# Seven modulation units of the second block's first layer move from TensorE to VectorE

## The chip, the cores and the metric

The kernel runs on one core of a Trainium2 chip. Its engines are TensorE (PE: matmuls, and PEld: the loading of the stationary operand), VectorE (DVE), ScalarE (ACT), GpSimd (POOL), and SyncE (SP), which here issues the loads from device memory. The metric is the device time of one execution in microseconds (us), the median of several runs; less is better.

## The reference, cut to what matters

Two transformer blocks of two layers each run one after the other on 256 latent tokens of width 1024, in float32. The second block also carries 256 context tokens through its first layer and is modulated: each of its layers computes six vectors of 1024 values for the latent tokens and six for the context from a condition vector, and these shift and scale the norms and gate the residual sums.

```python
for l in range(2):                       # second block
    mod_l = split(silu(c)     @ ada_w[l] + ada_b[l], 6)   # 1024 x 6144 weights
    mod_c = split(silu(c_ctx) @ ada_w[l] + ada_b[l], 6)
    hl = modulate(x_lat, norm_g[l, 0], mod_l[0], mod_l[1])
    hc = modulate(x_ctx, norm_g[l, 0], mod_c[0], mod_c[1])
    mix_c, mix_l = mixer(hc, hl, ...)    # l = 0: mLSTM + window attention; l = 1: global + neighbourhood
    x_lat = x_lat + mod_l[2] * (mix_l @ w_out[l])
    x_lat = x_lat + mod_l[5] * conv_ffn(modulate(x_lat, norm_g[l, 1], mod_l[3], mod_l[4]), ...)
    # x_ctx likewise with mod_c, in layer 0 alone
```

The condition vectors do not depend on the tokens, so the modulation can be computed at any time before its use, also while the first block runs.

## The kernel before, in words

**Stages.** The program is one long list of steps: attention 0 (to 160.7 us of the profiled span, where the next stage's first `gr` stands), the first block's FFN 0 (to 333), attention 1 (to 478), FFN 1 (to 694), the second block's first mixer (mLSTM heads 0 to 3 with their transposed outputs at 786.3, 825.1, 860.9 and 890.8, window attention and output projections, to 961), its FFN (to 1309), the second mixer (to 1520) and the last FFN.

**Weights.** All matmul weights come in units of at most 128 x 1056 floats, in the order of their first use (`fetch`, from L481). Each unit is loaded by SP into a `raw` buffer, split by ACT into a rounded high part `wh` (L496) and by DVE into the low part `wl` (L497), each with four buffers, and PE multiplies three products, high by high, high by low and low by high (L501). So each weight unit costs an instruction of about a microsecond on ACT and on DVE, and PE runs behind them by some units.

**Modulation.** Layer 0's 6144 columns are 24 units of 256 columns (the second layer has 24 more). A unit is computed in one of two ways. On PE (`p_ada`, from L599; the units named in `ADA_PE`, 13 to 19): two weight units are fetched and split, 16 matmuls 256 wide multiply them with the condition (`csil`), ACT copies the row (`adarow`, L616), two small matmuls turn it into columns, and DVE adds the bias (L621). On DVE (`ada_upto`, from L567): the unit is two blocks of 128 columns, whose transposed weights (`adaw`, 128 x 1024) SP loads unsplit, and for each block DVE runs two reductions over 1024 elements (L591), one for the latent and one for the context condition. These have three `adaw` buffers, two in FFN 1.

**Where the units stand.** The table `ADA` says how many units each slot takes, in order: slots `a0.0` to `a0.3` are woven into the four groups of attention 0, `f0` into FFN 0, `f1` into FFN 1, `e.0` to `e.2` into mLSTM heads 0 to 2 of the second block, and `f2` into its FFN. `ada_need` (L564) adds what a later step cannot do without: FFN 0's side list begins with `ada_need(0, 8)`, then the context's norm and modulation (`ctx_norm`), then slot `f0`.

**The order.** The program is built with `schedule_with_timeline_sim=True`: at build time a scheduler reorders the instructions of each engine by its own estimate of their times, with the list of steps as priority. A change of one step so moves others around it. On the chip each engine works through its list strictly in order.

**The mLSTM heads.** `core` (L1479) and `decay` (L1431) of a head are a chain: NM transposes on PE, W on DVE and ACT, W times the scores on DVE, the products `o` on PE, `hs` on DVE, a power on POOL, `hs` again, and the transposes `ht` (L1527). Beside head h stand steps that do not depend on it (`fill`): projections of the next heads, output projections, PE's modulation units, and beside head 3 the projections of the window attention's q.

Of the kernel before, what the change touches and what calls it, by code (L numbers as in the profile page):

```python
# [36 lines left out]

UNITS_AHEAD = 4
RAW_BUFS = 4
ADA_PE = range(13, 20)  # L40
HI_BUFS = 4
LO_BUFS = 4
CUTS = 1
# [4 lines left out]
def _ar(a, n):  # L48
    return np.arange(a, a + n)
# [6 lines left out]
def unit_specs():  # L56
# [7 lines left out]
    def halves(key, w, l, cols):  # L64
        for kh in range(2):
            add(key + (kh,), w, l, _ar(512 * kh, 512), cols)
# [12 lines left out]

    for i in ADA_PE:  # L80
        halves(("ada", 0, i), "ada_w_2", 0, _ar(256 * i, 256))
# [225 lines left out]
def weave(a, b, tail=0):  # L307
# [7 lines left out]


ADA = {
    "a0.0": 0, "a0.1": 1, "a0.2": 1, "a0.3": 2, "f0": 1, "f1": 4, "e.0": 3, "e.1": 2, "e.2": 2, "f2": 28,
}


# [55 lines left out]
class Prog:  # L377
# [189 lines left out]
    def ada_upto(self, n, room=True):  # L567
# [3 lines left out]
        for i in range(a, self.ada_at):  # L571
            if i in ADA_PE:
                out += self.p_ada(i // 24, i % 24)
# [1332 lines left out]
```

## Time and profile before

| | us |
|---|---|
| median of three runs | 1708.85 (1705.65 to 1709.5) |
| the profiled execution's own time | 1709.56 |
| its span, first to last instruction | 1707.8 |
| PE, PEld, DVE, ACT, POOL busy in the span | 1653.7, 1561.7, 1373.0, 953.9, 59.0 |

The span is what the trace covers; 1.8 us lie outside it. A matmul's record is longer than the distance to the next matmul's start, since matmuls are pipelined; what a matmul costs a busy PE is that distance. The same holds to a lesser degree of DVE.

### The profile page before, as it was taken

Reading aid. Unit: us, or ns where it says so; the run is one execution under the profiler, and the core shown is the slowest. Engines: PE = TensorE matmul, PEld = TensorE weight load, DVE = VectorE, ACT = ScalarE, POOL = GpSimd, SP = SyncE. Lnnn points to the kernel's source line nnn. Section 1 sums busy time; section 2 is a strip of 40 time slices with the busy share of each in tenths; the row PEclk is TensorE's granted clock in tenths of the full one; section 3 lists DMA queues with packets and bytes.
Section 4 is the critical chain, followed back from the end, with each engine's and each line's share of the span. In section 5 each row is a group of like instructions: output and inputs, shape, how many; then the busy total and the mean of one; then the engine's idle time right before and its main releaser. Section 6 shows DMA issues by size and latency. Waiting matters only on the chain.

```text
span 1707.8 us, 31978 instructions
## 1 busy us (share of the span) xinstructions
PE 1653.7 (97%) x12336; PEld 1561.7 (91%) x12336; DVE 1373.0 (80%) x2832; ACT 953.9 (56%) x1693; POOL 59.0 (3%) x75
## 2 busy tenths in 40 slices
PE   7999999999899999999989999999999999999999
PEld 7999999999899999899978997888889999899999
DVE  6798999887787887767687788998887864679887
ACT  6666555656677667555446653233335554666554
POOL 0000000000100000100010000000000210000000
PEclk9999999999999999999989999999999999999999
DMA  8446675554455564524421454757745521235663
GB/s 308 134 140 232 219 239 190 180 173 138 137 173 162 186 197 147 165 73 157 140 75 42 154 176 151 231 180 235 264 151 158 197 82 57 75 112 173 191 193 124
DMA packets 80664, 277.97 MB, mean 163 GB/s; under 512 B 8960, under 2 KB 12160, under 8 KB 80256
## 3 DMA queue, kind: packets, MB, share of 16 engines
q1 hardware_dynamic: 79216, 273.30, 49.6%
q10 hardware_dynamic: 1296, 2.62, 0.4%
q8 instruction: 97, 1.59, 0.4%
q14 instruction: 55, 0.45, 0.1%
HBM read 274.84 MB, written 1.05 MB: 162 GB/s over the span
## 4 chain that ended last, share of the span: by engine, by line
PE 62%; DVE 6%; ACT 3%; issue 1%; POOL 0%; DVEq 0%; ACTq 0%; POOLq 0%
PE acc L501 41%; PE s L501 15%; PE o L501 4%; DVE wl L497 2%; PE ptp L821 1%; ACT wh L496 1%; ACT L1028 1%; DVE nt L1145 0%; DVE cc L1026 0%; PE stv L501 0%; POOL rs L661 0%; PE tt L741 0%; ACT L1380 0%; PE tt L837 0%; DVE g L640 0%
## 5 line engine op out<-in xcount | busy, mean ns | idle before, releaser
L496 ACT ACTIVATE wh<-raw 128x1024 fp32r<-128x1024 f32 (+4 forms) x446 | 454.0, 1025 | 443.9 <-PE acc L501 291.3
L497 DVE TENSOR_TENSOR wl<-raw,wh 128x1024 fp32r<-128x1024 f32 (+4 forms) x446 | 524.6, 1181 | 114.1 <-ACT wh L496 111.2
L501 PE MATMUL acc<-nh,wh 128*128 128x256 f32 (+2 forms) x872 | 268.0, 308 | 4.2 <-DVE ug L1618 1.9
L501 PE MATMUL acc<-nh,wl 128*128 128x256 f32 (+2 forms) x872 | 268.1, 308 | 0.8 <-DVE wl L497 0.7
L501 PE MATMUL acc<-nl,wh 128*128 128x256 f32 (+2 forms) x872 | 266.6, 306 | 0.0
L501 PE MATMUL acc<-wh,nh 128*128 128x256 f32 (+2 forms) x768 | 220.5, 288 | 12.1 <-ACT nh L642 7.9
L501 PE MATMUL s<-nh,wh 128*128 128x256 f32 (+2 forms) x744 | 224.2, 301 | 0.9 <-ACT wh L496 0.9
L501 PE MATMUL s<-nh,wl 128*128 128x256 f32 (+2 forms) x744 | 223.4, 300 | 0.0
L501 PE MATMUL s<-nl,wh 128*128 128x256 f32 (+2 forms) x744 | 223.1, 300 | 0.0
L501 PE MATMUL acc<-wh,nl 128*128 128x256 f32 (+2 forms) x768 | 219.5, 288 | 2.2 <-DVE nl L1148 2.1
L501 PE MATMUL acc<-wl,nh 128*128 128x256 f32 (+2 forms) x768 | 218.7, 286 | 0.3 <-DVE wl L497 0.3
L501 PE MATMUL acc<-g,wh 128*128 128x256 f32 x1056 | 187.1, 281 | 5.2 <-ACT g L639 2.7
L501 PEld LDWEIGHTS acc<-nh,wh 128*128 128x128 f32 x872 | 164.2, 188 | 13.6 <-ACT nh L1147 2.1
L501 PEld LDWEIGHTS acc<-nh,wl 128*128 128x128 f32 x872 | 164.1, 188 | 10.0 <-DVE wl L497 1.4
L501 PEld LDWEIGHTS acc<-nl,wh 128*128 128x128 f32 x872 | 164.2, 189 | 8.3
L591 DVE CUSTOM_DVE_ANT_0 junk<-adaw,sil,c0t 128x1024 f32<-128x1024 f32 x132 | 168.8, 1278 | 0.2
L501 PEld LDWEIGHTS acc<-g,wh 128*128 128x128 f32 x1056 | 160.3, 189 | 7.7 <-ACT g L639 3.6
L501 PEld LDWEIGHTS acc<-wh,nh 128*128 128x128 f32 x768 | 147.6, 192 | 14.0 <-ACT nh L642 8.2
L501 PEld LDWEIGHTS acc<-wh,nl 128*128 128x128 f32 x768 | 147.7, 193 | 4.5 <-DVE nl L1148 3.0
L501 PEld LDWEIGHTS acc<-wl,nh 128*128 128x128 f32 x768 | 147.4, 192 | 1.3 <-DVE wl L497 0.7
L501 PEld LDWEIGHTS s<-nh,wh 128*128 128x128 f32 x744 | 139.8, 188 | 7.4 <-ACT wh L496 1.1
L501 PEld LDWEIGHTS s<-nl,wh 128*128 128x128 f32 x744 | 139.9, 188 | 6.1
(385 smaller groups left out, 3338.9 us busy)
## 6 DMA issues: line engine op xcount, KB each, us to landing
raw<-in_wts SPq DMA_DIRECT2D x342, 512.0 KB, 4.1
adaw<-in_ada SPq DMA_DIRECT2D x82, 512.0 KB, 4.4
raw<-in_wts SPq DMA_DIRECT2D x72, 448.0 KB, 3.4
raw<-in_wts SPq DMA_DIRECT2D x24, 384.0 KB, 3.1
x<-in_x SPq DMA_DIRECT2D x8, 256.0 KB, 6.6
raw<-in_wts SPq DMA_DIRECT2D x4, 408.0 KB, 3.5
rpb<-in_rpb ACTq DMA_DIRECT2D x1, 1536.0 KB, 8.8
raw<-in_wts SPq DMA_DIRECT2D x2, 528.0 KB, 3.9
```

The costliest lines, as they stand in the source:

```text
L496: nc.scalar.activation(hf[:, c], raw[:, c], AF.Copy)
L497: self.last_wl = nc.vector.tensor_sub(lf[:, c], raw[:, c], hf[:, c].bitcast(F32)).ins
L501: self.nc.tensor.matmul(o, a, b, start=start, stop=stop)
L591: self.nc.vector.tensor_tensor_reduce(out=junk, in0=tiles[j], in1=self.sil[:, c], scale=1.0, scalar=self.C["adab%d" % l][:, m:m + 1], op0= ...
L821: self.nc.tensor.transpose(pt[:, kb], P[:, kb * 128:(kb + 1) * 128], self.ident)
L1028: nc.scalar.activation(cc, cc, AF.Silu)
```

## The change

`ADA_PE` becomes empty, so no unit of the modulation is computed on PE, and `ADA` gives the seven units to DVE in earlier slots:

```diff
-ADA_PE = range(13, 20)
+ADA_PE = ()
 ADA = {
-    "a0.0": 0, "a0.1": 1, "a0.2": 1, "a0.3": 2, "f0": 1, "f1": 4, "e.0": 3, "e.1": 2, "e.2": 2, "f2": 28,
+    "a0.0": 2, "a0.1": 2, "a0.2": 2, "a0.3": 2, "f0": 4, "f1": 8, "f2": 28,
 }
```

| units computed in | attention 0 | FFN 0 | FFN 1 | mixer 1 (PE before) | FFN of the second block |
|---|---|---|---|---|---|
| before | 4 | 5 (4 by `ada_need`) | 4 | 7 | 28 |
| now | 8 | 4 | 8 | 0 | 28 |

Since eight units are done by the end of attention 0, `ada_need(0, 8)` adds nothing, and `ctx_norm` is the first step of FFN 0's side list. From the second block's FFN on, units and steps are the same.

In the built program DVE has 160 reductions of L591 where it had 132, and 14 fewer `wl`; ACT has 14 fewer `wh` and 7 fewer `adarow`; PE has 112 matmuls with `csil` and 14 small ones with `adarow` fewer. Reductions on DVE between the same neighbours of the program (the `on` of L833 and the `gr` of L1023, at these times in the trace of before):

| stretch | 55.1 to 82 | to 111 | to 138.2 | to 160.7 | to 190.5 | to 277.4 | 488.3 to 523.2 | to 560.3 | to 668.4 |
|---|---|---|---|---|---|---|---|---|---|
| before | 0 | 7 | 9 | 0 | 5 | 11 | 2 | 4 | 10 |
| now | 9 | 9 | 12 | 2 | 2 | 10 | 6 | 6 | 20 |

The first place is DVE at the end of attention 0, around the last pair of heads' `on` (L833), whose transposes become the last part of the mix (`mixl3`) and release the last output projection, whose sums are the L843 rows. Before:

```order
L831 RECIPROCAL rec_1792<-rsum_1524 128x4
L843 TENSOR_TENSOR x3_80<-x3_80,acc_1859 128x256
L497 TENSOR_TENSOR wl_1856<-raw_1853,wh_1855 128x1024
L833 TENSOR_TENSOR on_1794<-o_1523,rec_1792 128x256
L640 TENSOR_TENSOR mixl3_175<-tt_1796,mixh3_171 128x256
L843 TENSOR_TENSOR x0_77<-x0_77,acc_1885 128x256
L843 TENSOR_TENSOR x0_77<-x0_77,acc_1897 128x256
```

And now:

```order
L843 TENSOR_TENSOR x3_80<-x3_80,acc_1899 128x256
L497 TENSOR_TENSOR wl_1896<-raw_1893,wh_1895 128x1024
L831 RECIPROCAL rec_1832<-rsum_1564 128x4
L591 ISA junk_1606,mods0_148<-adaw_1596,sil_131,c0t_87 128x1024
L591 ISA mods0_148 128x1
L833 TENSOR_TENSOR on_1834<-o_1563,rec_1832 128x256
L591 ISA junk_1645,mods0_148<-adaw_1601,sil_131,c0t_87 128x1024
```

One reduction stands directly ahead of that `on`, and two more follow it, one of them ahead of `mixl3` and one behind it.

The second place is PE in mLSTM head 3, from its second group of NM transposes on (`wh_11210` with `nh` is the projection of the window attention's q, `exh` and `exl` with `wh_11193` the output projection of heads 0 and 1, `o` the products of head 3). Before:

```order
L1441 MATMUL NM_11335<-c0t_87,an_5856 128x128 x4
L501 MATMUL acc_11556<-wh_11210,nl1_141 128x256
L501 MATMUL acc_11556<-wh_11210,nh2_134 128x256
L501 MATMUL acc_11556<-wl_11211,nh2_134 128x256
L501 MATMUL acc_11556<-wh_11210,nl2_142 128x256
L501 MATMUL o_11415<-vx_11021,W_11318 128x129 x2
L501 MATMUL acc_11556<-wh_11210,nh3_135 128x256
```

And now:

```order
L1441 MATMUL NM_11167<-c0t_87,an_5886 128x128 x4
L501 MATMUL acc_11506<-exl_11096,wh_11193 128x512
L501 MATMUL acc_11506<-exh_11095,wl_11194 128x512
L501 MATMUL acc_11540<-exl_11096,wh_11193 128x512
L501 MATMUL acc_11540<-exh_11095,wl_11194 128x512
L501 MATMUL o_11247<-vx_10927,W_11150 128x129 x2
L501 MATMUL acc_11575<-exh_11095,wh_11193 128x512
L501 MATMUL acc_11575<-exl_11096,wh_11193 128x512
L501 MATMUL acc_11575<-exh_11095,wl_11194 128x512
L501 MATMUL o_11247<-vx_10927,W_11150 128x129
```

All 77 matmuls of the q projections that stood between the transposes `ht` of head 2 and of head 3 now stand ahead of head 2's, in the places that the `csil` matmuls have left.

## Rows read from the trace of the kernel before

**Rows 1.** The page's part 1: busy us, share of the span, instructions.

```profile
PE 1653.7 (97%) x12336; PEld 1561.7 (91%) x12336; DVE 1373.0 (80%) x2832; ACT 953.9 (56%) x1693; POOL 59.0 (3%) x75
```

**Rows 2.** Busy time by stretch, attention 0 and FFN 0; columns in its first line.

```profile
core 0: us, PE busy (x) PEld busy (x) DVE busy (x) ACT busy (x) POOL busy (x), PEclk, DMA share, GB/s
55.10:82.00 26.90, 26.90 (x233) 26.90 (x232) 16.90 (x40) 18.94 (x44) 0.00 (x0) 1.00 0.42 137
82.00:111.00 29.00, 29.00 (x253) 29.00 (x252) 25.37 (x57) 19.25 (x44) 0.00 (x0) 1.00 0.47 146
111.00:138.20 27.20, 25.88 (x217) 24.77 (x215) 26.68 (x66) 16.03 (x37) 0.00 (x0) 1.00 0.56 178
138.20:160.70 22.50, 20.54 (x171) 19.85 (x171) 17.98 (x39) 15.72 (x31) 1.96 (x2) 1.00 0.66 232
160.70:190.50 29.80, 29.30 (x258) 29.30 (x259) 29.80 (x56) 18.63 (x29) 0.00 (x0) 1.00 0.73 232
190.50:277.40 86.90, 85.52 (x740) 84.61 (x740) 81.50 (x146) 47.00 (x69) 0.87 (x1) 1.00 0.67 216
```

**Rows 3.** Busy time by stretch, FFN 1.

```profile
488.30:523.20 34.90, 33.45 (x279) 32.41 (x278) 32.31 (x76) 28.32 (x46) 0.00 (x0) 1.00 0.53 180
523.20:560.30 37.10, 34.41 (x277) 33.76 (x277) 27.86 (x55) 23.38 (x38) 0.00 (x0) 0.95 0.53 167
560.30:668.40 108.10, 105.53 (x897) 104.03 (x896) 89.01 (x177) 80.45 (x122) 0.00 (x0) 1.00 0.55 176
```

**Rows 4.** Busy time by stretch, mLSTM heads 1 to 3 and what follows.

```profile
786.30:825.10 38.80, 38.80 (x274) 36.02 (x273) 24.52 (x60) 18.98 (x42) 1.11 (x2) 1.00 0.37 121
825.10:860.90 35.80, 35.46 (x254) 33.03 (x253) 29.66 (x77) 16.92 (x38) 1.01 (x1) 1.00 0.35 118
860.90:890.80 29.90, 23.72 (x162) 21.08 (x160) 24.58 (x81) 14.51 (x38) 3.08 (x3) 0.93 0.27 89
890.80:943.90 53.10, 51.10 (x342) 45.34 (x342) 39.12 (x122) 28.78 (x64) 1.17 (x1) 0.94 0.12 41
```

**Rows 5.** PE's timeline in mLSTM: start us, length us, operation, count.

```profile
766.80 0.28 PE L501 MATMUL acc<-wl,csil 128*128 128x256 f32 x1
766.92 0.28 PE L501 MATMUL acc<-wh,csil 128*128 128x256 f32 x1
...
772.64 0.50 PE L501 MATMUL acc<-c0t,adarow 128*128 128x2 f32 x4
773.00 0.36 PE L501 MATMUL acc<-wl,csil 128*128 128x256 f32 x1
```

**Rows 6.** A group of PE from 764 to 848: busy us, mean ns; idle before.

```profile
L501 PE MATMUL acc<-wl,csil 128*128 128x256 f32 x56 | 14.0, 285 | 0.0
```

**Rows 7.** Groups of ACT and of DVE from 764 to 848.

```profile
L496 ACT ACTIVATE wh<-raw 128x1024 fp32r<-128x1024 f32 x24 | 25.1, 1056 | 28.8 <-PE acc L501 25.0 <-DVE mods L621 1.3 <-DVE wl L497 1.3
...
L497 DVE TENSOR_TENSOR wl<-raw,wh 128x1024 fp32r<-128x1024 f32 x24 | 29.1, 1223 | 6.8 <-ACT wh L496 6.0 <-PE acc L501 0.6
```

**Rows 8.** DVE's timeline in attention 0: a reduction and its read.

```profile
115.28 1.28 DVE L591 CUSTOM_DVE_ANT_0 junk<-adaw,sil,c0t 128x1024 f32<-128x1024 f32 x1
116.48 0.08 DVE L591 DVE_READ_ACCUMULATOR2_ANT mods<- 128x1 f32 x1
```

**Rows 9.** Waits from 55 to 191: us in total, times, longest.

```profile
DVE wl L497 <- ACT wh L496: 11.3, 11, 2.9
```

**Rows 10.** Groups from 860.9 to 890.8, head 3.

```profile
L501 PE MATMUL acc<-wh,nh 128*128 128x256 f32 x26 | 7.4, 285 | 0.0
...
L497 DVE TENSOR_TENSOR wl<-raw,wh 128x1024 fp32r<-128x1024 f32 x5 | 6.1, 1220 | 0.7 <-ACT wh L496 0.6
```

**Rows 11.** Busy time in slices of 10 us, around head 3's end.

```profile
880.00:890.00 10.00, 7.14 (x33) 5.55 (x31) 7.42 (x36) 3.07 (x13) 0.64 (x1) 0.84 0.00 0
890.00:900.00 10.00, 8.42 (x31) 6.50 (x32) 9.15 (x25) 4.23 (x10) 1.97 (x2) 0.66 0.00 0
```

**Rows 12.** Groups of DVE from 256 to 268, the context's modulation.

```profile
L1145 DVE SCALAR_TENSOR_TENSOR nt<-x,gs,bc 128x256 f32<-128x256 f32 x8 | 3.5, 474 | 0.0
```

## The prediction, made before the changed kernel ran

> **What bounds the kernel now.** I read the page's busy times first, then the busy times of stretches, then timelines. The page says PE 97% busy and its weight loads 91%, DVE 80%, ACT 56% [rows 1]: on average TensorE is the bound, and work that leaves it should pay. The average hides stretches with another bound, and this change takes work out of one and puts it into others.
>
> In the mLSTM heads, which the seven units leave, PE has no gap through head 1 (38.80 of 38.8) and almost none through head 2 (35.46 of 35.8), while DVE is busy for 24.52 and 29.66 [rows 4]. There PE decides. Head 3 is otherwise: PE 23.72 of 29.9, DVE 24.58 of 29.9 [rows 4]: neither is full, a chain between them decides.
>
> In attention 0, which gains eight blocks, PE is full until 111 and DVE is not: 16.90 of 26.9, then 25.37 of 29.0. From 111 to 138.2 it is turned round: DVE 26.68 of 27.2, and PE misses 1.3. In FFN 0 DVE has no free moment up to 190.5 (29.80 of 29.8), after that 81.50 of 86.9, with PE at 85.52 [rows 2]. FFN 1, which also gains eight blocks, has more room on DVE: idle 2.6 of 34.9, 9.2 of 37.1 and 19.1 of 108.1 us, PE nearly full [rows 3].
>
> **What the change removes.** A `csil` matmul's record is 285 ns long, 56 of one kind and 56 of the other [rows 6], which would make 32 us. But they start 0.12 us apart [rows 5], and that is what a full PE gets back: 112 x 0.12 = 13.4. The row's four small matmuls take 0.36 from start to start [rows 5], seven times 2.5. Together 15.9 us of PE. Beside it go 14 splits on ACT (1056 ns) and on DVE (1223 ns) [rows 7], 14.8 and 17.1 us, off the path in heads 1 and 2, where both engines have gaps. Weights of as many bytes are now loaded as `adaw`; DMA is at 0.27 to 0.73 of its time in all stretches concerned [rows 2 to 4], and the loads run ahead by several buffers, so I price them at nothing; where this cover fails, SP's list stands still at an `adaw` whose buffer DVE has not read, and the weights behind it come late, which would add to the DVE terms below.
>
> **What the heads give back.** PE is full only as long as there is something to fill it with. The scheduler has put other projections where the `csil` matmuls stood, and takes them from later. Counted in the program's order with the distance above (narrow is a matmul 256 columns wide, wide one of 512):
> - Up to head 0's transposes: 48 `csil` go, 43 narrow and 9 wide projection matmuls come: nothing.
> - Head 1: 32 `csil` and their small ones go, 38 narrow and 3 wide come, 9 wide go: 1.3 less. PE is without a gap before and should be after: -1.3.
> - Head 2: 32 `csil`, the small ones, 4 narrow and 3 wide go, 5.9 less: PE 29.6 where it had 35.46. But DVE keeps its conversions and needs 29.66 [rows 4]. With both at about 30, waits between them show; I take 32 for 35.8: -4. Bounds: -5.9 by PE alone; nothing, if the 6 us that DVE waits now stay beside 29.66.
> - Head 3: the 77 matmuls of the q projections go (9.3 us; a third of them is the row of 26 in [rows 10]), and with them 5 conversions of DVE, 6.1 us [rows 10]. PE then has 14.4, DVE 18.5. DVE waits now for 29.9 - 24.58 = 5.3; if that stays, the head takes 23.8: -6. [...] I charge 1 us: -5. Bounds: -8 (DVE's 18.5 and 3.4 us of waits) and +5.1 (the clock falls to half for the whole head and its 14.4 us all lie on the chain: 14.4 more, less the 9.3 that PE no longer has to do).
>
> Sum -10.3, bounds -15.9 (all of PE's work) and +3.8 (head 1's -1.3, nothing in head 2, +5.1 in head 3). What follows head 3 stands in the same order as before, and I change nothing there.
>
> [...]
>
> **What attention 0 pays.** One reduction occupies DVE for 1.20 us (115.28 to 116.48), though its record is 1.28 long; with the read behind it I count 1.21 [rows 8]. By the counts in the table of the change:
> - 55.1 to 82: 9 more, 10.9 us, where DVE is idle for 10.0 [rows 2]: 0.9 over. That idle time is mostly conversions that wait for ACT, 11.3 us between 55 and 191 [rows 9], and these waits shrink as DVE falls behind.
> - 82 to 111: 2 more, 2.4, into 3.6 idle.
> - 111 to 138.2: 3 more, 3.6, into 0.5.
>
> Together 16.9 into 14.1: DVE needs 85.9 us where 83.1 are. If it never waited, the last pair's `on` would come 2.8 later. If every present wait stayed, 16.9 later. DVE does best at 98% (111 to 138.2) and 94% (190.5 to 277.4) [rows 2]; at 96% the 85.9 become 89.5: 6.4 late. PE cannot cover this: behind `on` come the last part of the mix, the output projection, the sums and the norm, all before FFN 0's first matmul, so what is late there is late for good. Two more reductions follow `on`, 2.4 us, in a stretch with 4.5 us idle [rows 2] and half hidden by the transposes: 0.5. FFN 0's start has the context's modulation now, 16 instructions of some 0.4 us start to start (474 ns records, [rows 12]), 6.4, against 3 reductions fewer, 3.6: 2.8 more on a full DVE; PE runs behind conversions by some units and takes this up, about 1 us of it shows. Later FFN 0 loses that modulation, and with it most of the 1.4 us that PE misses from 190.5 to 277.4 [rows 2]: -1. I take +6.5 for all this; bounds 2.8 (no wait is left) and 16.9 (every wait stays).
>
> **What FFN 1 pays.** 16 more, 19.4 us, into 30.9 idle. Only the first stretch is over: 4 more, 4.9, into 2.6 [rows 3], 2.3 over; the stretch after has 9.2 idle and gets 2.4. The third goes from 89.01 to 101.1 of 108.1, 94%, a load at which FFN 0's PE misses 1.6% [rows 2]. PE there misses 2.6 now. +2, bounds 0 and 6 (all of the overflow, and 3.5 more of PE's waits in the third stretch).
>
> **Sum.** -10.3 + 6.5 + 2 = -1.8 on the profiled execution's 1709.56: 1707.8. The median of the runs lies 0.7 below that execution, so the median of the changed kernel should be 1707. Two large terms of opposite sign nearly cancel; that is the forecast.
>
> **Rivals.**
> 1. *All of PE's work comes back.* TensorE is 97% busy, DVE 80% [rows 1]. [...] By rows: heads -14, attention 0 only its overflow 2.8, FFN 1 nothing: 1698 on the median's scale. For it: the scheduler knows the new lists and fills DVE's gaps. Against it: head 3 was not PE's before, and 111 to 138.2 is DVE's.
> 2. *DVE becomes the bound of attention 0*, the other side. The place is the last pair's `on`; it decides from the point where DVE's waits between 55.1 and 138.2 stay above 7 us beside the 16.9 added. Then `on` is 10 late, FFN 0's start 2 more, and with FFN 1 at 4 and the heads at -8 the kernel takes 8 longer: 1717. For it: DVE is at 98% before the three reductions come, the softmax of four heads runs through it, and each pair of reductions is 2.4 us in which nothing else gets done. Against it: PE has no gap up to 111 while DVE waits [rows 2], so that a DVE that falls a little behind starves nobody there at first.
> 3. *The heads' chain eats the gain.* Head 3, bared of its fill, stays at 29.9 because of the clock, and head 2 at 34: heads -3, the rest as in the forecast: +5.5, 1714. For it: the clock of 0.66 [rows 11]. Against it: the chain there is mostly DVE's, and DVE loses 6.1.
>
> **How the numbers follow.** Changes under 0.2%, 3.4 us, cannot be told from none by measuring this kernel. Forecast, 1701 to 1712 about 1707: 0.50 (faster 0.19, same 0.30, slower 0.01). Rival 1, 0.20, faster. Rival 2, 0.20, slower. Rival 3, 0.10, same 0.03 and slower 0.07. Faster 0.39, same 0.33, slower 0.28. The range from 1696 to 1719 takes in both rivals' centres and leaves a tenth at each end.
>
> **What would show it.** In the changed profile: no `csil` matmul on PE; head 1 still without a PE gap; head 2 at 31 to 33 us with PE and DVE both above 90%; head 3 at 24 to 26, PE near 14 us busy and its clock under 0.9. FFN 0's first `gr` at 165 to 169 instead of 160.7, with DVE above 95% busy from 60 on. FFN 1 longer by 0 to 4. I am wrong if that first `gr` comes before 163 or after 172, if head 3 does not get shorter, or if PE's gaps in FFN 1 grow by more than 6.

## The result and the profile after

The changed kernel takes 1715.86 us, the median of five runs (1713.81 to 1716.56); the kernel before took 1708.85 (1705.65 to 1710.87) beside it. The medians lie 7.0 us apart. The ratio on record, which is not the quotient of these two medians, is 1.0052, 95% interval 1.0034 to 1.0071: about 9 us slower (6 to 12), where 1.8 us faster were forecast.

On the page of the changed kernel PE's busy time fell by 9 us against [rows 1], DVE's rose by 13, and the span grew (the mean granted clock of the profiled execution fell from 0.989 to 0.982):

```profile
span 1712.0 us, 31693 instructions
PE 1645.0 (96%) x12196; PEld 1550.5 (91%) x12196; DVE 1386.2 (81%) x2867; ACT 932.5 (54%) x1668; POOL 59.0 (3%) x75
```

Busy times of attention 0 and FFN 0 after, cut at the same instructions as [rows 2] (columns as there: the stretch, its length, busy us of PE, PEld, DVE, ACT, POOL, granted clock, DMA):

```profile
53.10:84.50 31.40, 30.84 (x264) 30.70 (x264) 29.43 (x65) 22.68 (x50) 0.00 (x0) 1.00 0.60 196
84.50:111.50 27.00, 27.00 (x235) 26.91 (x233) 25.51 (x61) 17.15 (x43) 0.00 (x0) 1.00 0.56 179
111.50:141.40 29.90, 25.82 (x206) 23.80 (x205) 29.90 (x70) 15.55 (x35) 0.00 (x0) 0.98 0.64 212
141.40:164.70 23.30, 22.40 (x171) 21.79 (x171) 20.52 (x47) 15.22 (x32) 1.97 (x2) 0.88 0.57 199
164.70:198.20 33.50, 33.00 (x289) 33.00 (x289) 32.53 (x67) 23.96 (x39) 0.70 (x1) 1.00 0.55 179
198.20:282.30 84.10, 82.68 (x710) 81.41 (x709) 74.32 (x125) 42.01 (x59) 0.00 (x0) 1.00 0.67 223
```

DVE is now full from 111.5 to 141.4 without a break, PE misses 4.1 us there, and the last pair's `on` comes at 141.4 and FFN 0's first `gr` at 164.7, where they were at 138.2 and 160.7. In the stretch behind `on` the granted clock was 0.88 where it was 1.00 [rows 2]; that stretch is only 0.8 longer, 23.3 for 22.5. FFN 0's first stretch takes 33.5 for 29.8; later FFN 0 gives part back, as forecast: 84.1 for 86.9.

FFN 1 after, as [rows 3], and the heads, as [rows 4]:

```profile
493.70:529.80 36.10, 32.10 (x256) 31.19 (x255) 35.70 (x80) 23.38 (x36) 0.00 (x0) 0.95 0.60 191
529.80:568.30 38.50, 36.31 (x308) 35.87 (x309) 31.65 (x64) 25.25 (x44) 0.00 (x0) 1.00 0.61 190
568.30:672.00 103.70, 100.92 (x867) 99.81 (x866) 95.43 (x187) 74.30 (x115) 0.00 (x0) 1.00 0.62 204
...
792.50:829.70 37.20, 37.20 (x267) 34.67 (x266) 19.98 (x55) 14.67 (x37) 1.11 (x2) 1.00 0.18 58
829.70:868.10 38.40, 31.64 (x206) 28.73 (x204) 26.54 (x70) 15.57 (x36) 1.43 (x2) 0.90 0.34 110
868.10:893.90 25.80, 17.21 (x83) 13.88 (x83) 19.78 (x77) 9.59 (x32) 2.59 (x3) 0.82 0.00 1
```

Head 1 is 1.6 shorter and still full of PE work, head 3 is 4.1 shorter. Head 2 is the surprise: it lost 32 `csil` matmuls and took 38.4 us for 35.8, with PE idle for 6.8 and DVE for 11.9 (0.3 and 6.1 before). Neither engine bounds it by its sum. Slices of 5 us of head 2, first before, then after, show where the idle time lies:

```profile
825.10:830.10 5.00, 5.00 (x46) 5.00 (x45) 4.26 (x9) 3.01 (x8) 0.00 (x0) 1.00 0.30 105
830.10:835.10 5.00, 5.00 (x45) 5.00 (x44) 3.41 (x12) 3.03 (x11) 0.00 (x0) 1.00 0.02 3
...
855.10:860.90 5.80, 5.80 (x36) 5.08 (x35) 5.34 (x16) 1.76 (x5) 1.01 (x1) 1.00 0.23 90
```

```profile
829.70:834.70 5.00, 5.00 (x31) 4.26 (x29) 4.81 (x11) 4.18 (x11) 0.00 (x0) 1.00 0.53 163
834.70:839.70 5.00, 5.00 (x27) 4.18 (x26) 5.00 (x14) 2.76 (x7) 0.00 (x0) 1.00 0.12 47
839.70:844.70 5.00, 5.00 (x32) 4.40 (x31) 5.00 (x16) 1.89 (x4) 0.00 (x0) 1.00 0.32 108
844.70:849.70 5.00, 5.00 (x39) 4.73 (x39) 2.88 (x7) 1.06 (x1) 0.00 (x0) 1.00 0.31 105
849.70:854.70 5.00, 5.00 (x46) 5.00 (x45) 3.43 (x8) 2.17 (x3) 0.00 (x0) 1.00 0.50 149
854.70:859.70 5.00, 3.29 (x29) 3.08 (x27) 2.36 (x6) 2.12 (x2) 0.00 (x0) 1.00 0.26 79
859.70:864.70 5.00, 3.35 (x14) 3.08 (x14) 1.43 (x5) 0.69 (x4) 0.00 (x0) 0.57 0.60 193
864.70:868.10 3.40, 0.00 (x0) 0.00 (x0) 1.62 (x9) 0.69 (x4) 1.43 (x2) 0.50 0.00 0
```

Before, the head's end is full. After, DVE is nearly full in the first 15 us (14.81), PE has no gap for 28 us, and in the last 8.4 PE is busy for 3.35 and DVE for 3.05. The group that fills DVE from 829.7 to 845 is the sums of the output projection of heads 0 and 1, beside three conversions:

```profile
L857 DVE SCALAR_TENSOR_TENSOR x<-acc,mods,x 128x256 f32<-128x256 f32 x16 | 6.9, 475 | 0.0
L497 DVE TENSOR_TENSOR wl<-raw,wh 128x1024 fp32r<-128x1024 f32 x3 | 3.7, 1219 | 0.6 <-ACT wh L496 0.6
```

In the kernel before these 16 sums stood in the second half of the head, behind the chain's first `hs`; now they stand ahead of it. DVE's timeline, first before, then after (start us, length us, engine, line, operation, count):

```profile
835.68 0.42 DVE L1512 TENSOR_TENSOR hs<-o,dn 128x256 f32<-128x256 f32 x1
...
846.32 0.87 DVE L857 SCALAR_TENSOR_TENSOR x<-acc,mods,x 128x256 f32<-128x256 f32 x2
```

```profile
844.05 0.87 DVE L857 SCALAR_TENSOR_TENSOR x<-acc,mods,x 128x256 f32<-128x256 f32 x2
...
846.69 0.43 DVE L1512 TENSOR_TENSOR hs<-o,dn 128x256 f32<-128x256 f32 x1
```

So the head's chain reaches its first `hs` 17.0 us into the head instead of 10.6. PE does not stand still for that: up to about 858 it runs fill, the q projections above all, in the order of its list, which the trace keeps on PE throughout (12196 matmuls). When only the chain's last products are left, that fill is used up, and the tail runs alone. Its timeline (as above, with the idle time before and what ended it):

```profile
859.12 1.23 DVE L497 TENSOR_TENSOR wl<-raw,wh 128x1024 fp32r<-128x1024 f32 x1 [0.19 <-ACT wh L496]
860.26 0.60 DVE L1515 SCALAR_TENSOR_TENSOR hs<-o,dn,hs 128x128 f32<-128x128 f32 x2
...
861.01 3.35 PE L501 MATMUL o<-vx,W 128*128 128x129 f32 x14 [3.02 <-DVE hs L1515]
864.40 0.16 DVE L1506 COPY d<-o 128x2 f32<-128x2 f32 x1 [3.54 <-PE o L501]
...
868.12 0.48 PE L1527 MATMUL ht<-c0t,hs 128*128 128x128 f32 x1 [3.76 <-DVE hs L1526]
```

A conversion stands ahead of `hs`, PE's last products wait for `hs` and then take 3.35 us (14 of them, with a granted clock of 0.50 from 861.0 to 864.4), and then DVE, ACT and POOL finish while PE has nothing. Before, the last 14 took 1.72 us, with a granted clock of 1.00 there:

```profile
851.55 1.72 PE L501 MATMUL o<-vx,W 128*128 128x129 f32 x14
```

### The profile page after: what moved, and what is told of

It is laid out like the page before. It is cut to its first block, busy times and chain, and to the rows that moved or that the text cites. A ratio compares the mean times of both kernels' runs of the same rounds, so it can differ in the third digit from the quotient of the medians.

```text
span 1712.0 us, 31693 instructions
## 1 busy us (share of the span) xinstructions
PE 1645.0 (96%) x12196; PEld 1550.5 (91%) x12196; DVE 1386.2 (81%) x2867; ACT 932.5 (54%) x1668; POOL 59.0 (3%) x75
## 4 chain that ended last, share of the span: by engine, by line
PE 63%; DVE 6%; ACT 2%; issue 1%; POOL 0%; ACTq 0%; DVEq 0%; POOLq 0%
PE acc L501 41%; PE s L501 15%; PE o L501 4%; PE ptp L821 2%; DVE wl L497 1%; DVE junk L591 1%; ACT wh L496 0%; DVE cc L1026 0%; POOL rs L661 0%; ACT L1380 0%; DVE nt L1145 0%; PE stv L501 0%; ACT sm L1380 0%; PE tt L741 0%; PE tt L837 0%
## 5 line engine op out<-in xcount | busy, mean ns | idle before, releaser
L496 ACT ACTIVATE wh<-raw 128x1024 fp32r<-128x1024 f32 (+4 forms) x432 | 439.2, 1025 | 453.3 <-PE acc L501 306.4
L497 DVE TENSOR_TENSOR wl<-raw,wh 128x1024 fp32r<-128x1024 f32 (+4 forms) x432 | 506.4, 1178 | 102.2 <-ACT wh L496 100.0
L501 PE MATMUL acc<-wh,nh 128*128 128x256 f32 (+2 forms) x768 | 219.2, 286 | 11.9 <-ACT nh L642 7.6
L591 DVE CUSTOM_DVE_ANT_0 junk<-adaw,sil,c0t 128x1024 f32<-128x1024 f32 x160 | 204.2, 1276 | 0.3
```

The source lines that it names most:

```text
L496: nc.scalar.activation(hf[:, c], raw[:, c], AF.Copy)
L497: self.last_wl = nc.vector.tensor_sub(lf[:, c], raw[:, c], hf[:, c].bitcast(F32)).ins
L501: self.nc.tensor.matmul(o, a, b, start=start, stop=stop)
L591: self.nc.vector.tensor_tensor_reduce(out=junk, in0=tiles[j], in1=self.sil[:, c], scale=1.0, scalar=self.C["adab%d" % l][:, m:m + 1], op0= ...
```

## The experiments

Of each edit the lines that matter are shown.

Theory A: the heads gave almost nothing, because the scheduler filled PE's new room with fill from later and left the tails bare; the rest is the price in attention 0, as forecast, and in FFN 1. Rival B: the heads gave the forecast's 10 us, and attention 0 cost far more than it shows. All comparisons are with the kernel before, run beside each kernel on the same chip. The two traces alone would not do: the first `on` of attention 0 came between 52.6 and 55.5 us in the profiles. So stage lengths were read from all of them, from the first instruction to FFN 0's first `gr`, from there to FFN 1's first, from there to FFN 1's last sum (`x` of L843), to `ht` of head 0, to `ht` of head 3, and to the end:

```
                         to FFN 0  to FFN 1  FFN 1   to ht 0   head 1  head 2  head 3   rest
before                     160.7     327.6   201.4     96.6     38.7    35.9    29.9    817.0
heads_alone                158.3     328.3   202.1     95.4     37.1    38.2    27.5    816.6
attn0_alone                164.6     326.8   200.4     94.0     38.7    35.9    27.5    817.6
ffn1_alone                 161.3     327.3   211.9     95.1     38.8    36.1    27.6    817.3
no_ffn1                    165.3     328.0   200.7     93.6     37.2    38.3    25.4    816.2
changed                    164.7     329.0   203.1     95.7     37.2    38.4    25.8    818.1
oa3                        166.4     327.7   204.9     95.2     38.0    33.1    27.2    818.5
hold_q                     164.9     327.8   206.6     96.8     37.2    28.7    31.0    820.8
warm3                      166.6     327.4   204.8     95.7     37.2    38.4    31.1    815.8
f1_eight                   160.4     328.2   208.1     94.4     37.9    40.9    26.7    822.0
f1_all                     159.7     331.3   206.2     95.6     37.1    38.2    27.0    818.1
before_oa3                 159.7     329.1   200.3     94.0     38.7    36.0    34.2    818.5
a0_six                     162.1     325.5   199.0     95.1     38.8    36.0    28.7    817.5
a0_early                   162.2     324.6   202.3     94.2     38.8    36.2    27.3    820.7
```

**One part at a time.** `heads_alone` leaves the seven units out:

```diff
             if i in ADA_PE:
-                out += self.p_ada(i // 24, i % 24)
+                continue
```

> The kernel before without its seven PE units, whose modulation is left at zero (part of the computation is left out); attention 0, FFN 0 and FFN 1 are as before, and the heads' order on PE is nearly that of the changed kernel. Theory A (the heads give back little, because PE's order leaves the tail of head 2 bare): from ht of head 0 to ht of head 3 101 to 102 us where before has 104.5, head 2 at 37 to 39, and the whole 2 to 4 us faster than before. Rival B (the heads give what was forecast, and attention 0 cost more than it shows): 10 us faster, 94 to 95 us between these two ht.

Measured: ratio 1.0000 (0.9986 to 1.0013). Taking 15.9 us of PE work, 14 conversions and their loads out of the heads, and putting nothing anywhere, gains nothing that can be measured; at the interval's end it is 2.4 us. Rival B is out, and theory A's 2 to 4 us faster was too much as well; from `ht` to `ht` the profile has 102.8, where 101 to 102 were expected. Head 2 does the same as in the changed kernel:

```profile
784.10:821.20 37.10, 37.10 (x266) 34.61 (x265) 19.95 (x55) 14.65 (x37) 1.11 (x2) 1.00 0.17 58
821.20:859.40 38.20, 31.47 (x206) 28.69 (x204) 26.53 (x70) 15.63 (x36) 1.41 (x2) 0.95 0.33 110
859.40:887.00 27.60, 19.21 (x84) 15.36 (x84) 20.15 (x77) 9.70 (x32) 2.68 (x3) 0.75 0.00 1
```

`attn0_alone` puts the new load on attention 0 and FFN 0 and nowhere else:

```diff
-    "a0.0": 0, "a0.1": 1, "a0.2": 1, "a0.3": 2, "f0": 1, "f1": 4, "e.0": 3, "e.1": 2, "e.2": 2, "f2": 28,
+    "a0.0": 2, "a0.1": 2, "a0.2": 2, "a0.3": 2, "f0": 1, "f1": 4, "e.0": 3, "e.1": 2, "e.2": 2, "f2": 28,
...
+                if i == 8:
+                    blocks += 3 * [(-1, 2 * i), (-1, 2 * i + 1)]
```

(-1 stands for a second computation of the block into a scratch tile.)

> The kernel before with eight units in attention 0 and four in FFN 0, three of these computed a second time into a scratch tile: up to the end of FFN 0 the instructions of the changed kernel, behind it those of the kernel before. Theory A: 4 to 6 us slower than before, the first gr of FFN 0 at 164 to 165, the first gr of FFN 1 some 5.5 late. Rival B: 8 to 10 slower. If attention 0 cost only what DVE has over (2.8), FFN 0 would start at 163.5 and the whole be 3 slower.

Measured: 1.0023 (1.0013 to 1.0034), 4 us, with FFN 0's first `gr` at 164.6: as theory A had it. The first `gr` of FFN 1 came only 3.1 later than before, not 5.5.

`ffn1_alone` puts it on FFN 1 alone, with each of its four units computed a second time:

```diff
                 blocks += [(i // 24, 2 * (i % 24)), (i // 24, 2 * (i % 24) + 1)]
+                if not room:
+                    blocks += [(-1, 2 * i), (-1, 2 * i + 1)]
```

> The kernel before with each of FFN 1's four units computed a second time into a scratch tile, so 32 reductions in FFN 1 as in the changed kernel, all else as before. Theory A: under 1.5 us slower (the trace of the changed kernel shows +0.7 between the first gr of FFN 1 and ht of head 0). The forecast's term: 2 slower. Rival C (FFN 1 is where the rest of the loss is, hidden in one profile by chance): 4 or more slower.

Measured: 1.0060 (1.0048 to 1.0073), 10 us; every expectation but rival C's is missed. Its FFN 1 up to the ninth `gr` (560.3 before, 572.6 here) holds the same 141 instructions on DVE, 12 reductions among them, as the changed kernel's, but in another order:

```profile
488.70:525.70 37.00, 31.59 (x241) 30.22 (x240) 33.66 (x75) 23.20 (x37) 0.00 (x0) 0.91 0.52 175
525.70:572.60 46.90, 41.86 (x319) 40.93 (x319) 33.70 (x69) 26.14 (x44) 0.00 (x0) 0.89 0.52 163
```

That is 83.9 us for the changed kernel's 74.6 and 72.0 before. The waits of its stretch from 501 to 573 (engine, line, what it waited for, us in total, times, longest; `sm` of L1383 stands at L1380 in the kernel before) show a convoy with the context's window attention, whose scores and softmax (`s`, `sm`) stand in this stage too:

```profile
ACT wh L496 <- PE s L501: 13.9, 4, 5.5
...
PE s L501 <- ACT sm L1383: 5.3, 2, 3.7
```

Before, ACT's conversions waited 2.0 us for `s` there, in the changed kernel 5.5 (506 to 568.3). The granted clock was 0.91 and 0.89 here, 1.00 and 0.95 before [rows 3], so part of the 12 us can be slower matmuls. No wait for a load stands in that list. So the reductions' number does not set FFN 1's cost alone; the order that the scheduler makes of it does as well. So this run does not isolate the changed kernel's FFN 1, as it was meant to. For that `no_ffn1` was run, the changed kernel less the four units that FFN 1 got:

```diff
-    "a0.0": 2, "a0.1": 2, "a0.2": 2, "a0.3": 2, "f0": 4, "f1": 8, "f2": 28,
+    "a0.0": 2, "a0.1": 2, "a0.2": 2, "a0.3": 2, "f0": 4, "f1": 4, "f2": 28,
...
+            if 16 <= i < 20:
+                continue
```

> The changed kernel without the four units that came new into FFN 1 (four units' modulation is left at zero, so part of the computation is left out): attention 0 and FFN 0 as changed, FFN 1 with 16 reductions in the order that it has behind the changed FFN 0, the heads bare. Theory A (attention 0 and FFN 0 cost 4, the heads give nothing): 3 to 5 us slower than before; what the changed kernel has beyond that, some 3 us, is FFN 1's. If the heads and attention 0 together carry all of the loss: 7 to 9 slower.

Measured: 1.0025 (1.0013 to 1.0037), 4 us, as theory A had it. The changed kernel's remaining 4 to 5 us are FFN 1's (4.6 by the two ratios; by their intervals 1 to 8).

`f1_eight` repeats the order of `ffn1_alone` with real units:

```diff
-ADA_PE = range(13, 20)
+ADA_PE = range(17, 20)
...
-    "a0.0": 0, "a0.1": 1, "a0.2": 1, "a0.3": 2, "f0": 1, "f1": 4, "e.0": 3, "e.1": 2, "e.2": 2, "f2": 28,
+    "a0.0": 0, "a0.1": 1, "a0.2": 1, "a0.3": 2, "f0": 1, "f1": 8, "e.0": 1, "e.1": 1, "e.2": 1, "f2": 28,
```

> The kernel before with only four units moved: FFN 1 takes eight on DVE, the three that are left stay on PE, one each beside heads 0 to 2; attention 0 and FFN 0 as before. FFN 1's instructions on DVE stand in the same order as in the run with the units computed twice, not in that of the changed kernel. Theory E (FFN 1's cost is the order that the scheduler finds for its first 80 us, not the number of reductions): again 9 to 12 us lost between the first and the ninth gr of FFN 1, about 8 to 10 slower than before in all. Theory F (16 reductions cost what DVE has over, and the run before was a chance): +1 in FFN 1, in all 0 to 2 slower.

Measured: 1.0087 (1.0068 to 1.0106), 15 us. 79.9 us up to the ninth `gr`, 8 more than before: the order's cost came again, a little under theory E's 9 to 12, and theory F is out. The granted clock up to that `gr` was 0.96. `ffn1_alone`, with the same instructions in the same order on PE, DVE and ACT, took 4 more there at 0.91 and 0.89. The rest is not FFN 1's: head 2 took 40.9, and what follows head 3 822 instead of 817, which the expectation did not have.

`f1_all` puts all seven units into FFN 1 (`ADA_PE = ()`, `"f1": 11`, attention 0 as before):

> All seven units go into FFN 1, with attention 0 and FFN 0 as before and no modulation on PE: 44 reductions in FFN 1 where the changed kernel has 32, its third order there. By count alone, 28 reductions more are 34 us into 31 us of DVE's idle time before: 3 to 8 us lost there, the heads give 0 to 3 back, so 2 to 6 slower than before. If attention 0 is what matters (rival B): 3 or more faster than before. If the order in FFN 1 decides, anything from 0 to 12 slower.

Measured: 1.0040 (1.0026 to 1.0054), 7 us, a little over the count's 2 to 6. Attention 0 untouched, and still slower than before: rival B falls a second time. With 44 reductions FFN 1 takes 206.2, less than with 32 in the order of `ffn1_alone`.

**Where the fill stands in the heads.** `oa3` gives the scheduler the output projection of heads 0 and 1 one slot later:

```diff
-    "att0": 'd', "q0": '3', "att1": 'd', "q1": '3', "oa": '2', "ol": 'd', "tail": 4, "mix": 0, "cm": 'e',
+    "att0": 'd', "q0": '3', "att1": 'd', "q1": '3', "oa": '3', "ol": 'd', "tail": 4, "mix": 0, "cm": 'e',
```

> The changed kernel with the output projection of heads 0 and 1 put into the list one slot later, beside head 3; the program still does 48 of its matmuls and 93 of the q projections' in head 2, but the q projections first and the output projection at the tail. Theory A (the tail of head 2 is bare because of where the fill stands): PE has no gap over 2 us in head 2, which takes 31 to 34 us instead of 38.4, and 2 to 5 us are gained over the changed kernel, 1711. Rival D (head 2 is the sum of what its chain and DVE must do): 37 to 39 as changed.

`hold_q` instead keeps the q projections behind `ht` of head 2:

```diff
-            fill[EV["q%d" % i]] += proj_q(i, True)
+            fill[EV["q%d" % i]] += self.behind("ht2", proj_q(i, True))
```

> The changed kernel with the 96 matmuls of the window attention's q projections held behind the transposes ht of head 2, so that they fill head 3; all else as changed. Theory A (where the fill lies decides): head 2 at 26 to 31 us where the changed kernel has 38.4, head 3 at 30 to 34 where it has 25.8, the two together 58 to 62 instead of 64.2, and 2 to 6 us faster than the changed kernel, about 1711. Rival D (the chains of heads 2 and 3 have a fixed sum, and fill only moves it): 64 for both, and 1716 as changed.

Heads 2 and 3 of `oa3`, then of `hold_q`:

```profile
832.10:865.10 33.00, 28.86 (x197) 26.30 (x195) 26.23 (x68) 14.42 (x35) 1.41 (x2) 1.00 0.41 128
865.10:892.40 27.30, 16.95 (x88) 12.81 (x88) 22.79 (x86) 10.35 (x33) 3.85 (x3) 0.87 0.00 1
```

```profile
833.30:862.00 28.70, 19.74 (x111) 15.99 (x109) 21.32 (x64) 10.19 (x30) 1.01 (x1) 1.00 0.21 74
862.00:893.00 31.00, 25.83 (x180) 23.50 (x180) 24.80 (x82) 14.64 (x37) 3.30 (x3) 0.95 0.20 68
```

`oa3` does all but a few of the same matmuls in head 2, with the sums later and the output projection at the tail, and needs 33.0 for 38.4: the forecast's 32, nearly. That the order decides, as theory A has it, is so shown; rival D had 37 to 39. The tail is still bare, though: PE has nothing for the last 4.1 of the 33.0, where no gap over 2 was expected. The edit moved two things at once, the sums (the first `hs` comes 10.7 into the head again) and the fill, so what each costs is not separated. In `hold_q` the sums stay where the changed kernel has them and the first `hs` comes at 17.0 again, but without the q projections ahead of them the last products come at 23.2 instead of 31.3, and the head takes 28.7: the sums' place alone does not make head 2 long. The two heads together take 60.3 in `oa3`, 59.7 in `hold_q`, as expected, and 64.2 as changed. Of the time little comes through: `oa3` 1.0032 (1.0018 to 1.0046), 1712.6 us, whose interval overlaps the changed kernel's, and `hold_q` 1.0056 (1.0040 to 1.0073), no better than the changed kernel, which misses the expectation for the whole: what it gains in the heads it gives back, 820.8 us behind head 3 instead of 818.1, and a longer FFN 1 with the same order.

`before_oa3` is the same one-slot edit on the kernel before:

> The kernel before, with its seven PE units, and the output projection of heads 0 and 1 one slot later in the list; most of the q projections' matmuls so come into head 2 and 36 more matmuls of the output projection into head 3. Theory A (heads 2 and 3 together hold 65.7 us because of where the fill stands): 3 to 5 us less for the two, 2 to 4 us faster than before in all. Rival I (with the PE units there the heads are full of work and the place of the fill is indifferent): within 2 us of before.

Measured: 1.0043 (1.0028 to 1.0059), slower, against both expectations. Heads 2 and 3:

```profile
821.80:857.70 35.90, 35.90 (x295) 35.15 (x294) 26.68 (x65) 19.93 (x42) 2.61 (x2) 1.00 0.40 133
857.70:892.00 34.30, 23.57 (x125) 17.90 (x123) 30.02 (x102) 12.47 (x35) 2.64 (x2) 1.00 0.16 61
```

There head 2 is full of PE work in either order, and with the sums that came into head 3 DVE is its fullest engine (30.0 of 34.3, PE 23.6). In these two pairs the edit shortened heads 2 and 3 where PE had run out of fill, and lengthened them where it had not.

`warm3` asks what the low granted clock of the bare head 3, 0.82, costs. It adds 96 matmuls on operands at hand, into a bank that nobody reads:

```diff
+            if k == "3":
+                fill[k] += self.behind("ht2", sum([warm(12) for _ in range(8)], []))
```

> The changed kernel with 96 matmuls of 256 columns beside head 3, on operands that lie ready and into a bank that nobody reads: PE work without weights, conversions or sums, 11.5 us at full clock, and nothing else; up to ht of head 2 PE's order is that of the changed kernel. Theory G (head 3 is held by the low clock that comes with its bareness): the granted clock of head 3 rises from 0.82 to above 0.95, the head takes 21 to 24 us instead of 25.8, and what follows is not longer. Theory H (it is held by the chain over DVE, ACT and POOL, and the clock costs little): 25 to 28 us in spite of the full clock, and the whole 0 to 2 slower than the changed kernel.

```profile
870.10:901.30 31.20, 26.80 (x184) 25.38 (x184) 23.58 (x86) 10.52 (x33) 3.81 (x3) 0.88 0.01 1
```

Measured: 1.0080 (1.0063 to 1.0097). The clock rose only from 0.82 to 0.88, and the head took 5.3 us more, not less: H's 25 to 28 is missed, since half of the 11.5 us of added PE work shows, and G's numbers are missed too; but its condition, a clock above 0.95, was not met, so G is not refuted by this run. The profiles of the other kernels say something on it. Head 3 of `no_ffn1`:

```profile
863.00:888.40 25.40, 15.86 (x84) 12.51 (x84) 19.70 (x77) 9.75 (x32) 2.63 (x3) 0.88 0.01 1
```

Head 3 took 25.4 at a granted clock of 0.88 here, 25.8 at 0.82 in the changed kernel, 27.0 at 0.81 in `f1_all` and 27.5 at 0.75 in `heads_alone`, with the same instructions, but in orders that differ somewhat, on DVE most. It is so longer by up to 2 us where the clock is lower; that the clock is the cause, and what the head would take at full clock, no run shows.

**A better split.** `a0_six` leaves the heads and FFN 1 alone and moves two units from FFN 0's full start to the first half of attention 0; `a0_early` takes one more from its last group to its first:

```diff
-    "a0.0": 0, "a0.1": 1, "a0.2": 1, "a0.3": 2, "f0": 1, "f1": 4, ...
+    "a0.0": 1, "a0.1": 2, "a0.2": 1, "a0.3": 2, "f0": 1, "f1": 4, ...    # a0_six
+    "a0.0": 2, "a0.1": 2, "a0.2": 1, "a0.3": 1, "f0": 1, "f1": 4, ...    # a0_early
```

> The kernel before with two more units in the first two groups of attention 0, where DVE has idle time, and two fewer at the start of FFN 0, where it has none: six units in attention 0 where before has four and the changed kernel eight; the heads and FFN 1 as before. If attention 0's price comes with the reductions behind 82 us (theory A): FFN 0's first gr at most 1 us later than before, FFN 1's first gr 1 to 4 us earlier, 1 to 3 us faster. If any reduction in attention 0 delays it (half of the changed kernel's 4): first gr 2 later, FFN 0 gives 2 back, and no difference.

> As the run with six units in attention 0, but with two in each of the first two groups and one in each of the last two, so that DVE has two reductions' pairs fewer where it is full (behind 82 us) and two more where it is not. Theory A (the price of attention 0 is the reductions behind 82 us): the first gr of FFN 0 0.5 to 1.5 us earlier than in that run, about 4 us faster than before. If what counts is the number of reductions ahead of the last on: no difference to that run, 2 to 3 us faster than before.

`a0_six`: 0.9983 (0.9973 to 0.9993), 1703.1 us, faster than both kernels by a little, and the only one that is. Its attention 0 and FFN 0, from the first `on` to FFN 1's neighbourhood:

```profile
55.40:83.70 28.30, 28.30 (x244) 28.30 (x243) 22.35 (x50) 20.86 (x49) 0.00 (x0) 1.00 0.50 175
...
140.10:162.10 22.00, 21.05 (x174) 19.98 (x172) 17.95 (x39) 15.35 (x32) 1.97 (x2) 1.00 0.65 233
...
193.20:277.30 84.10, 83.98 (x733) 83.58 (x732) 73.66 (x130) 45.57 (x66) 0.86 (x1) 1.00 0.62 207
```

FFN 0 starts 1.4 later than before, where at most 1 was expected (1.1 counted from the first `on`, which scatters), and is level with it at 277.3, with PE full (83.98 of 84.1); FFN 1's first `gr` comes 0.7 earlier, where 1 to 4 were expected. The time is theory A's, the stages lie between its numbers and the other theory's. `a0_early` came to 1.0003 (0.9990 to 1.0015): its FFN 0 starts at the same 162.1, so one unit earlier buys nothing there, both expected times are missed, and theory A's point about 82 us is not borne out; up to FFN 1 its profile is even level with `a0_six`, and the difference arises in FFN 1 and behind head 3. The gain of `a0_six` is so small that I would not build on it.

## Why the prediction was wrong, point by point

The means of the table's columns, over the kernels that share an order in a stage, or nearly, give the sum; each row of the table is one execution. To FFN 0: 160.0 for six kernels with attention 0 as before, 165.4 for six with the changed one: +5.4. From there to FFN 1: 328.1 and 327.8, without `f1_all`, where work of the next stage stands ahead of its first `gr`: -0.3. FFN 1: 200.9 with 16 reductions (seven kernels), 204.8 in the changed kernel's order (four): +3.9. To `ht` of head 0, the same kernels: 94.7 and 95.9: +1.1. Heads 1 to 3: 103.0 with the PE units in the order of before (five kernels), 101.9 in the changed order (four, `f1_all` and `heads_alone` among them): -1.1. The rest: nothing beyond the scatter. Together +9.0; the timed difference is 0.52%, 8.9 (7.0 by the medians).

- **Attention 0 and FFN 0, +6.5:** right, +5.1. DVE at its limit around the last `on`, PE unable to cover, a smaller part given back later in FFN 0. From the first `on` to the last it is 83.0 to 83.1 in each of the six kernels with the order of before and 88.1 to 88.3 in each of the six with the changed one: +5.2, where 6.4 was charged, with DVE at 96% as charged (84.84 of 88.3). In FFN 0 two sizes were off and cancel, which is luck: its start cost 3.7 where 1 was charged, and 2.8 came back where 1 was. The first `gr` at 164.7 lies just under the 165 to 169 named; the time to the first `on`, 53.1 for 55.1, is 2.0 less there, for which no run shows a cause.
- **FFN 1, +2:** mis-sized, +3.9 in the stage and 5.1 up to head 0, inside its bounds of 0 to 6. It lies where the forecast put it: up to the ninth `gr` 72.0 became 74.6 to 76.1 in the four kernels of this order. That another order could cost 8 to 12 there was in no bound. Part of the 3.9 goes with the clock: at a granted clock of 0.99 over the stage the changed order took 203.1 and four kernels with 16 reductions (`before`, `attn0_alone`, `no_ffn1`, `before_oa3`) 200.3 to 201.4, which is near the forecast's 2; the last section has the rest.
- **Heads, -10.3: the step that failed.** Head 1 came as worked out (-1.3 forecast, 38.8 to 37.2). "Head 2: -4. Bounds: -5.9 ...; nothing" came out at +2.3 (36.0 to 38.3, in four kernels alike), outside its bounds. The step took the larger of PE's 29.6 and DVE's 29.66 and added 2 for waits, at most the 6 of before, so no order could make the head longer than before. (The 5.9 of removed PE work comes to 5.8 by the distances given there.) DVE's work came out smaller, 26.54, and its waits at 11.9; PE's work at 31.64, with 1.6 of it from the slow last products (3.35 us for 1.72), and its gaps at 6.8. A head is a chain, and fill helps only if it stands beside it. The two programs' order showed the q projections moving ahead of `ht` of head 2; I counted them and did not ask what stood last before that `ht`, nor where on DVE the 16 sums of the output projection had gone. `oa3` and `hold_q` show that the order of this work decides the head's length; how much is the sums' and how much the fill's stays open.
- **Head 3, -5:** -1.8 in the mean (28.2 to 26.4). The 29.9 of [rows 4] from which it was taken away is the longest of five profiles with this order on PE (27.3 to 29.9): 1.7 of the term was the chance of one execution: at a granted clock of 1.00 the same head took 27.3 to 27.6 in three profiles (`attn0_alone`, `ffn1_alone`, `a0_early`), at 0.94 28.7 in `a0_six`, and the 29.9 had 0.93 [rows 4]. The fear that head 3 would stay at 29.9 because of the clock did not come true either, though its granted clock fell to 0.82. No run shows the 1 us that was charged there for the clock: in orders near the changed one the head took 25.4 at a granted clock of 0.88, 25.8 at 0.82, 27.0 at 0.81 and 27.5 at 0.75. Half the clock, which the upper bound had for the whole head, was granted for a part of it: 0.50 from 880 to 883 before, from 868.1 to 877 after.
- **Removed conversions and loads at nothing:** not contradicted. `heads_alone` drops them together with PE's work and gains nothing, and in the changed kernel's waits from 53 to 191 and from 488 to 698 none of PE, DVE or ACT is for a load; no run moves the loads alone.
- **Rivals.** The first, all of PE's work coming back, is refuted most plainly by `heads_alone`. In head 2, where PE was busy for 35.46 of 35.8 [rows 4], the units' work is taken away from it there, and the head took 38.2, because its chain then ended it. The second gave 1717, near the time, and the measured time lies in the wide range; that is luck, for it is not by its mechanism: from the first `on` the last came 5.2 later, not 10. The third, the heads' chain eating the gain, is the right one; its size and place were wrong, -1.1 instead of -3, in head 2 instead of head 3, and its cause, the order of the work beside the chain instead of the clock.
- **What follows head 3** does not stand quite in the order of before: PE's order is the same for its first 669 of 5449 matmuls. The stage took 818.1 for 817.0, within the 815.8 to 822.0 of all the kernels.
- **The forecast of the time** is 10.8 off by the stage sums: 9.2 in the heads and 3.1 between FFN 1 and head 0, less 1.4 in attention 0, each rounded.

## What to carry to other kernels

Work taken from the fullest engine beside a dependent chain is worth only the time in which that chain is not what ends the stage; price it by asking what will stand last before the chain's end, on each engine, in the new order. If a scheduler rebuilds the order at every edit, an edit is also a new draw: here the same DVE work took 3 to 4 us more than before in one order of a stage and 8 to 12 in another. Before trusting a term of a few us read from one profile, look at the same stage in a second execution, with its granted clock.

## What was not expected of the hardware

`before` and `before_oa3` have the same instructions in the same order on PE and DVE up to the heads. The one met a fall of the granted clock at the start of the mixer, the other did not. The stretch 40 us behind the last `gr` of FFN 1, before and in `before_oa3`:

```profile
708.40:718.40 10.00, 10.00 (x53) 9.00 (x53) 6.94 (x15) 3.66 (x6) 0.00 (x0) 0.79 0.21 74
```

```profile
708.00:718.00 10.00, 9.73 (x59) 8.44 (x58) 7.30 (x17) 4.80 (x10) 0.00 (x0) 1.00 0.34 105
```

In the 10 us ahead, PE was busy for 7.19 us in both; the granted clock there was already 0.87 in the first, 1.00 in the second. From FFN 1's last sum to `ht` of head 0 the first took 96.6, the second 94.0 us. In this stage the profiles with a granted clock of 1.00 throughout took 93.6 to 94.2 (four kernels: `no_ffn1`, `attn0_alone`, `before_oa3`, `a0_early`), those in which it fell 94.4 to 96.8 (ten kernels), whatever their order. The same shows in FFN 1 between kernels with the same order of PE, DVE and ACT, the changed kernel and `hold_q`:

```profile
493.70:696.80 203.10, 194.07 (x1638) 191.22 (x1638) 184.69 (x373) 141.83 (x228) 0.31 (x1) 0.99 0.61 198
```

```profile
492.70:699.20 206.50, 197.28 (x1638) 194.36 (x1637) 185.18 (x373) 141.68 (x228) 0.26 (x1) 0.98 0.58 194
```

So the same work can cost 2 to 3 us more from one execution to another, and this goes with the granted clock; that is as much as several of the terms that were disputed here. It also leaves a question open: the changed kernel's clock is lower than before's, 0.982 for 0.989, and how much of its loss is gaps and how much is matmuls at a lower granted clock, no run here separates.
